# The second modulation of an encoder layer: its last sixth made inside the feed-forward stage

## The chip, the cores and the metric

The kernel runs on one core of a Trainium2 chip. The metric is the device time of one execution in microseconds. Three runs of the kernel before took 1530.63, 1531.85 and 1537.08 us; their median is 1531.85 us.

## What is computed

One layer of a hybrid encoder over a sequence of 1024 tokens of width 1024, all in float32. A conditioning vector `c` gives six vectors of width 1024 through one matrix; two of them scale and shift the input of the mixers, one gates the mixers' output, two scale and shift the input of the feed-forward part, and the last, `g2`, gates its output. Cut to what matters here:

```
cond = silu(c)
sh1, sc1, g1, sh2, sc2, g2 = split(cond @ mod_w + mod_b, 6)
h = rms_norm(x) * (1 + sc1) + sh1
y = concat(ssd(h @ w_in), attention(..), mlstm(..), hyena(..)) @ w_out
x = x + g1 * y
h = rms_norm(x) * (1 + sc2) + sh2
x = x + g2 * ((silu(h @ w_gate) * (h @ w_up)) @ w_down)
return rms_norm(x, final_norm_g)
```

So `g2` is needed only at the very end, when the product with `w_down` is complete, `g1` when `w_out` is prepared, and `sh2`, `sc2` before the feed-forward part.

## The kernel before, in words

The program is written as one sequence of stages, and a scheduler orders each engine's instructions at compile time: it goes by priority (the place in the program, earlier first; what stands under `K.first()`, L226, counts as 2000 places earlier) and by its own estimate of when an instruction's inputs are there. An instruction that is ready may therefore be placed long before the stage in which it is written. At run time every engine and the SP queue, which issues nearly all loads, keep the order that was fixed. A tile that takes the place of another (same tag or slot) waits until the last reader of the old one is done.

The stages, in order of time, are: `start` (the first modulation, the norm of the input) and the Hyena filters; the Hyena convolutions with the SSD and later input projections running beside them on TensorE (`hyena` L819, `project_ssd` L932, lines L493 and L505 for the projections' products); SSD; the mLSTM with the rest of the projections; attention and the output projection; the feed-forward part (`ffn` L1580).

**The second modulation.** The four vectors `g1`, `sh2`, `sc2`, `g2` are 4096 columns of the matrix, cut in eight parts `n` of 512 columns. `modulation2` (L1485) is a generator that `project_ssd` calls between its weight groups, two parts to a call; the fourth call is drained behind it. For each part it loads eight blocks of 128 rows (tile `mxw`, 128x512, 256 KB, two buffers, L1494), multiplies each by its column of `cond` and adds it up on VectorE (L1496 for the first, L1498 for the other seven) in `mxacc` (two buffers), and stores the 128x512 partial sums to memory (`macc`, L1499). Much later, between `project_ml` and `mlstm`, `modulation2_sums` (L1504) loads each `mxacc` again (L1510) and adds over the 128 partitions: for `sh2` and `sc2` by four transposes on TensorE and a reduction (L1514, L1516), for `g1` and `g2` by a product with a matrix of ones (L1527), which leaves the row on all partitions. A bias is added (L1528) and the row stored in `gd` (L1529). `g1` is loaded in `attention` (L1446), `g2` behind the block products (L1712).

**The Hyena stage beside it.** For each of nine frequencies VectorE makes a tile `yk`, TensorE transforms it (`fps`, L790 to L795), VectorE multiplies the result with the filter (L798 to L802, tiles `ta`, `tb`, `rt`), and TensorE transforms it back (`ips`, L804 to L809).

**The five block products.** The products with `w_gate` and `w_up` are computed in a Strassen-like form. A first loop over the 22 hidden blocks makes two block products (`Z`), stored to `psd`. The second loop makes five more: each is 12 matmuls of 128x128 by 128x512, 60 in a block `f`. They go to PSUM tiles `X` and `Y` in turn:

```
product(X, w["T2"], A["S2"], True)
V.tensor_tensor(u, X, p1, op=ALU.add)
product(Y, w["T1"], A["S1"], True)
V.tensor_tensor(v, Y, p1, op=ALU.add)
product(X, w["T3"], A["S3"], False)
V.tensor_tensor(v, X, v, op=ALU.add)
```

The third product adds into the `X` that `u` has read, so it can't begin before VectorE has read it; the same holds for `Y` and the fourth, and for `X` and the fifth. VectorE also makes the weights of block `f + 1` meanwhile (`weights`, L1664).

**Slots.** From attention on, SBUF is a set of numbered slots; a tile names one slot or a ring of several that it takes in turn. Slots 17, 18 and 21 are free in the second loop. `psr`, which holds what the first loop stored, goes round slots 27, 0, 1, 2. The down projection (`part`, L1720) takes slots 17, 18 and 21 first for its weights `wdr`, `wdh`, `wdl`; `g2` lies in slot 0. In the down projection each of eight accumulators takes three matmuls per hidden block: `ah` by `wdh`, `al` by `wdh`, `ah` by `wdl` (L1742).

Of the kernel before, what the change touches and what calls it, by code (L numbers as in the profile page):

```python
# [9 lines left out]
F32 = mybir.dt.float32  # L10
# [7 lines left out]
P = 128  # L18
# [267 lines left out]
def build(nc, tc, d, out, dbg=None, dump=None):  # L286
    K = Net(nc, tc, d, out)
    with ExitStack() as es:
# [43 lines left out]
        K.acr = dp.tile([64, P], F32, name="acr")  # L332
        K.macc = [dp.tile([P, 512], F32, name=f"macc{n}") for n in range(8)]
        K.gd = dp.tile([2, P, D], F32, name="gd")
        K.xd = [dp.tile([P, D], F32, name=f"xd{n}") for n in range(8)]
# [9 lines left out]
        with ExitStack() as e2:  # L345
# [3 lines left out]
            with ExitStack() as e3:  # L349
# [7 lines left out]
                for _ in hf:  # L357
                    pass
            mp = Tags(rpool("m2", right), mxw=2)
            m2 = modulation2(K, mp)  # L360
# [1016 lines left out]
def attention(K, sp, S):  # L1377
# [54 lines left out]
    for a in range(2):  # L1432
        yp = [S.tile([P, 2, 512], F32R, 42 + j, "ny") for j in range(2)]
        ys = [(y[:, 0], y[:, 1]) for y in yp]
        for ti in (2 * a, 2 * a + 1):
            for f in range(2):
                vw = S.tile([120, 4, 256], F32, (40, 41), "nvw")
                rr = NA_ROWS[ti][0]
                for n, cw in enumerate(NA_CH[NA_KIND[ti]]):
                    nc.sync.dma_start(vw[:cw * 40, n], K.vn[f, rr:rr + cw].rearrange("r c e -> (r c) e"))  # L1440
                    rr += cw
                for j in range(2):
                    unit(ti, f, j, vw)
                if ti == 0 and f == 0:
                    K.g1 = S.tile([P, D], F32, 18, "g1")
                    nc.sync.dma_start(K.g1, K.gd[0])  # L1446
            ss = sp.tile([P, 2, 2], F32, "fss", bufs=2)
# [37 lines left out]
def modulation2(K, sp):  # L1485
# [3 lines left out]
    mv = K.mod2  # L1489
    for n in range(8):  # L1490
        acc = sp.tile([P, 512], F32, "mxacc", bufs=2)
        for k in range(NK):
            mt = sp.tile([P, 512], F32, "mxw")
            nc.sync.dma_start(mt, d["modw2"][k * P:(k + 1) * P, n * 512:(n + 1) * 512])  # L1494
            if k == 0:
                V.tensor_scalar_mul(acc, mt, K.cond[:, 0:1])  # L1496
            else:
                V.scalar_tensor_tensor(acc, in0=mt, scalar=K.cond[:, k:k + 1], in1=acc, op0=ALU.mult, op1=ALU.add)  # L1498
        nc.sync.dma_start(K.macc[n], acc)  # L1499
        if n % 2:  # L1500
            yield


def modulation2_sums(K, sp):  # L1504
    nc, d = K.nc, K.d
    V = nc.vector
    mv = K.mod2
    for n in (0, 1, 6, 7, 2, 3, 4, 5):
        acc = sp.tile([P, 512], F32, "mxacc", bufs=2)
        nc.sync.dma_start(acc, K.macc[n])  # L1510
        if 2 <= n < 6:
            ps = K.pm.tile([P, 512], F32, tag="m", name="m2p")
# [8 lines left out]
        else:  # L1521
            m, h = n // 6, n % 2
            hs = slice(h * 512, (h + 1) * 512)
            bb = sp.tile([P, 512], F32, "mxw", name="mxb")
            nc.sync.dma_start(bb, d["modbg"][m:m + 1, hs].broadcast_to([P, 512]))
            ps = K.pm.tile([P, 512], F32, tag="m", name="mgp")
            nc.tensor.matmul(ps, lhsT=K.ones, rhs=acc, start=True, stop=True)  # L1527
            V.tensor_tensor(bb, bb, ps, op=ALU.add)  # L1528
            nc.sync.dma_start(K.gd[m][:, hs], bb)  # L1529

# [49 lines left out]
def ffn(K, sp, S, at):  # L1580
# [100 lines left out]
    with K.first():  # L1681
        ws = [weights(0)]
    for f in range(NF):
        ps1 = S.tile([P, 2, H], F32, (27, 0, 1, 2), "psr")
        nc.sync.dma_start(ps1, K.psd[f])
# [24 lines left out]

    g2 = S.tile([P, D], F32, 0, "g2")
    nc.sync.dma_start(g2, K.gd[1])  # L1712
    fg = S.tile([P, D], F32, 1, "fg")
    nc.sync.dma_start(fg, d["fing"].broadcast_to([P, D]))
    ss = sp.tile([P, 2, 8], F32, "ss")
    for dh in range(2):
# [3 lines left out]
        def part(f2):  # L1720
            raw = S.tile([P, 2, H], F32, (17, 9, 10, 11), "wdr")
            nc.sync.dma_start(raw, d["wd"].rearrange("(a b p) e -> a p b e", b=2, p=P)[f2, :, :, ds])
            wh = S.tile([P, 2, H], F32R, (18, 12, 13, 14), "wdh")
            wl = S.tile([P, 2, H], F32R, (21, 15, 16, 8), "wdl")
            K.split(wh, wl, raw)
# [60 lines left out]
```

## Time and profile before

| | us |
|---|---|
| median of three runs | 1531.85 |
| profiled execution | 1531.33 |
| its span, first to last instruction | 1529.5 |
| TensorE busy in the span | 1412.3 |
| VectorE busy in the span | 1043.3 |
| ScalarE busy in the span | 527.6 |
| GpSimd busy in the span | 91.4 |

The profiled execution took 1.8 us more than its span; what lies outside is the same for any version. PE is TensorE, PEld its weight loads, DVE VectorE, ACT ScalarE, POOL GpSimd, SP the queue that issues loads and stores. A row of a timeline gives start, duration, engine, line, operation, output and inputs, and in brackets how long the engine had been idle before and what ended that. "issue" as releaser means that the engine waited for nothing that the profile shows. The clock is the share of TensorE's full rate that was granted: 1.00 is 2.4 GHz, 0.50 is 1.2 GHz, and a mean between them is a mixture of both.

### The profile page before, as it was taken

What the parts mean: (1) busy time and instruction counts of PE and PEld (TensorE: products, weight loads), DVE (VectorE), ACT (ScalarE), POOL (GpSimd) and SP (SyncE); (2) the same over time, 40 slices, a digit from 0 to 9 for tenths busy, and PEclk for the clock granted to TensorE, in tenths of its full rate; (3) what the DMA queues carried; (4) which work ended last, traced back from release to release, by engine and by line L of the source; (5) the groups of instructions that cost most, each with busy time, mean ns of one, the idle gap of its engine ahead of it and who ended that gap; (6) DMA issues with size and microseconds to landing.
All of it is one profiled execution on the core that took longest, in us unless ns stands there. A gap on an engine that the chain in (4) does not pass through costs nothing.

```text
span 1529.5 us, 19231 instructions
## 1 busy us (share of the span) xinstructions
PE 1412.3 (92%) x6849; PEld 1141.0 (75%) x6849; DVE 1043.3 (68%) x2004; ACT 527.6 (34%) x958; POOL 91.4 (6%) x143
## 2 busy tenths in 40 slices
PE   2589979998998998989989999999999999999997
PEld 0366768876797777867767777888888888888886
DVE  7998977977847684687865476477777766335327
ACT  2522221232242342333456775322222223224222
POOL 2110000000102231230000000000000000000000
PEclk9789999999998999999999999999999999999999
DMA  6534467577653325476426457554444448643402
GB/s 247 194 104 143 128 197 230 185 225 226 190 185 110 105 87 155 125 265 203 154 87 217 150 170 276 201 180 164 148 144 153 149 164 305 222 149 123 153 1 110
DMA packets 134899, 257.02 MB, mean 168 GB/s; under 512 B 24703, under 2 KB 69663, under 8 KB 134804
## 3 DMA queue, kind: packets, MB, share of 16 engines
q1 hardware_dynamic: 111508, 228.50, 45.4%
q10 hardware_dynamic: 22688, 25.99, 4.8%
q0 software_dynamic: 608, 1.31, 0.3%
q8 instruction: 54, 0.88, 0.2%
q14 instruction: 41, 0.34, 0.1%
HBM read 195.17 MB, written 60.59 MB: 167 GB/s over the span
## 4 chain that ended last, share of the span: by engine, by line
PE 74%; DVE 13%; DMA 5%; issue 2%; ACT 2%; POOL 2%; SPq 0%; DVEq 0%; ACTq 0%; POOLq 0%
PE dps L1742 14%; PE X L1603 12%; PE gps L493 9%; PE Z L1603 8%; PE Y L1603 8%; PE gps L505 4%; PE gps L1554 3%; PE nS L1427 2%; PE ops L1554 1%; DMA mxw<-modw 1%; PE nS L1405 1%; DVE wlo L239 1%; PE kps L763 1%; PE mpa L1339 1%; DVE acc L422 1%
## 5 line engine op out<-in xcount | busy, mean ns | idle before, releaser
L1742 PE MATMUL dps<-wdh,ah 128*128 128x512 f32 x352 | 136.9, 389 | 0.0
L1742 PE MATMUL dps<-wdh,al 128*128 128x512 f32 x352 | 136.9, 389 | 0.0
L1742 PE MATMUL dps<-wdl,ah 128*128 128x512 f32 x352 | 136.9, 389 | 0.0
L493 PE MATMUL gps<-hhi,whi 128*128 128x512 f32 x320 | 130.7, 408 | 3.8 <-ACT nt L529 3.8
L493 PE MATMUL gps<-hlo,whi 128*128 128x512 f32 x320 | 129.6, 405 | 0.0
L493 PE MATMUL gps<-hhi,wlo 128*128 128x512 f32 x320 | 129.0, 403 | 0.0
L1603 PE MATMUL Z<-hp,wgh 128*128 128x512 f32 x352 | 95.4, 402 | 1.9 <-ACT ps L1658 1.6
L239 DVE TENSOR_TENSOR al<-ar,ah 128x1024 fp32r<-128x1024 f32 x44 | 53.4, 1222 | 47.9 <-ACT ah L233 47.9
L505 PE MATMUL gps<-whi,hhi 128*128 128x256 f32 (+1 forms) x256 | 77.5, 303 | 1.5 <-ACT z L529 1.5
L1603 PEld LDWEIGHTS Z<-hp,wgh 128*128 128x128 f32 x352 | 63.7, 188 | 19.8 <-ACT ps L1658 5.3
L505 PE MATMUL gps<-whi,hlo 128*128 128x256 f32 (+1 forms) x256 | 77.2, 302 | 0.0
L505 PE MATMUL gps<-wlo,hhi 128*128 128x256 f32 (+1 forms) x256 | 77.1, 301 | 0.0
L1742 PEld LDWEIGHTS dps<-wdl,ah 128*128 128x128 f32 x352 | 66.1, 188 | 13.8
L1742 PEld LDWEIGHTS dps<-wdh,al 128*128 128x128 f32 x352 | 66.1, 188 | 13.7
L1742 PEld LDWEIGHTS dps<-wdh,ah 128*128 128x128 f32 x352 | 66.1, 188 | 13.6
L493 PEld LDWEIGHTS gps<-hhi,whi 128*128 128x128 f32 x320 | 60.6, 189 | 19.5 <-ACT nt L529 5.0
L493 PEld LDWEIGHTS gps<-hhi,wlo 128*128 128x128 f32 x320 | 60.5, 189 | 13.8 <-issue 1.6
L233 ACT CAST ah<-ar 128x1024 fp32r<-128x1024 f32 x44 | 45.7, 1048 | 72.5 <-PE dps L1742 42.7
L493 PEld LDWEIGHTS gps<-hlo,whi 128*128 128x128 f32 x320 | 60.6, 189 | 12.4 <-issue 0.8
L1603 PE MATMUL X<-A,t4s 128*128 128x512 f32 x264 | 63.4, 389 | 0.0
L239 DVE TENSOR_TENSOR wdl<-wdr,wdh 128x1024 fp32r<-128x1024 f32 x22 | 26.9, 1224 | 53.1 <-ACT wdh L233 53.1
L1498 DVE SCALAR_TENSOR_TENSOR mxacc<-mxw,cond,mxacc 128x512 f32<-128x512 f32 x56 | 42.0, 750 | 29.2 <-DMA mxw<-modw 28.9
(500 smaller groups left out, 3240.5 us busy)
## 6 DMA issues: line engine op xcount, KB each, us to landing
wg<-wg SPq DMA_DIRECT2D x44, 512.0 KB
ar<-ad SPq DMA_DIRECT2D x44, 512.0 KB
mxw<-modw SPq DMA_DIRECT2D x64, 256.0 KB
raw<-w_in SPq DMA_DIRECT2D x28, 512.0 KB
psd<-ps SPq DMA_DIRECT2D x22, 512.0 KB
psr<-psd SPq DMA_DIRECT2D x22, 512.0 KB
wu<-wu SPq DMA_DIRECT2D x22, 512.0 KB
wdr<-wd SPq DMA_DIRECT2D x22, 512.0 KB
```

The lines of the kernel that those rows point to most:

```text
L233: nc.scalar.copy(hi, src)
L239: e.tensor_tensor(lo, src, hi.bitcast(F32), op=ALU.subtract)
L422: V.scalar_tensor_tensor(acc, in0=w, scalar=c, in1=acc, op0=ALU.mult, op1=ALU.add)
L493: nc.tensor.matmul(ps, lhsT=w[:, k, c], rhs=x[k][:, t], start=n == 0, stop=n == len(seq) - 1)
L505: nc.tensor.matmul(ps, lhsT=x[k][:, t], rhs=w[:, k, :N], start=n == 0, stop=n == len(seq) - 1)
L763: nc.tensor.matmul(ps, lhsT=tab[:, la], rhs=y[:, 0], start=True, stop=not cx)
L1339: nc.tensor.matmul(pa[:, 2 * j + dr], lhsT=sds[dr][:, h], rhs=va[:, h], start=True, stop=True)
L1427: nc.tensor.matmul(pb[:, 448:512], lhsT=pT[:w * 40, n], rhs=vw[:w * 40, n, c:c + 64], start=n == 0, stop=n == len(chunks) - 1)
L1498: V.scalar_tensor_tensor(acc, in0=mt, scalar=K.cond[:, k:k + 1], in1=acc, op0=ALU.mult, op1=ALU.add)
L1554: K.nc.tensor.matmul(ps, lhsT=l, rhs=r, start=n == 0, stop=n == 5)
L1603: nc.tensor.matmul(ps, lhsT=w[a][:, k], rhs=x[k][b], start=start and n == 0, stop=n == 11, skip_group_check=not start)
L1742: nc.tensor.matmul(acc[i], lhsT=x[:, ts], rhs=m, start=f == 0 and n == 0, stop=f == NF - 1 and n == 2)
```

## The change

The two parts `n` of `g2` leave `modulation2` and `modulation2_sums`; six parts remain. In these, `mxw` has three buffers in place of two and `mxacc` one in place of two (the same SBUF in all), and the parts are summed in the order 0 to 5. `g2` is now made in `ffn`, written at block `f == 4` of the second loop: eight loads of 128x1024 (512 KB) go round slots 18 and 21, VectorE adds them up in slot 17, the bias is loaded into the same ring, and two products with the ones matrix and two additions leave `g2` in slot 17, where it stays. Its way through memory (`macc`, `gd`) is gone. In the down projection the first slots of the rings are 18, 21 and 0 in place of 17, 18 and 21.

```diff
-            mp = Tags(rpool("m2", right), mxw=2)
+            mp = Tags(rpool("m2", right), mxw=3)
@@ modulation2 and modulation2_sums
-    for n in range(8):
-        acc = sp.tile([P, 512], F32, "mxacc", bufs=2)
+    for n in range(6):
+        acc = sp.tile([P, 512], F32, "mxacc")
...
-    for n in (0, 1, 6, 7, 2, 3, 4, 5):
-        acc = sp.tile([P, 512], F32, "mxacc", bufs=2)
+    for n in range(6):
+        acc = sp.tile([P, 512], F32, "mxacc")
@@ new
+def weighted_rows(K, S, c0, acc, slots):
+    nc, d = K.nc, K.d
+    for k in range(NK):
+        mt = S.tile([P, D], F32, slots, "mwt")
+        nc.sync.dma_start(mt, d["modw2"][k * P:(k + 1) * P, c0:c0 + D])
+        if k == 0:
+            nc.vector.tensor_scalar_mul(acc, mt, K.cond[:, 0:1])
+        else:
+            nc.vector.scalar_tensor_tensor(acc, in0=mt, scalar=K.cond[:, k:k + 1], in1=acc, op0=ALU.mult, op1=ALU.add)
+
+def modulation_g2(K, S, slots):
+    nc, d = K.nc, K.d
+    acc = S.tile([P, D], F32, slots[0], "g2")
+    weighted_rows(K, S, 3 * D, acc, slots[1:])
+    bb = S.tile([P, D], F32, slots[1:], "g2b")
+    nc.sync.dma_start(bb, d["modbg"][1:2].broadcast_to([P, D]))
+    for h in range(2):
+        hs = slice(h * 512, (h + 1) * 512)
+        ps = K.pg.tile([P, 512], F32, tag="g", name="mgp")
+        nc.tensor.matmul(ps, lhsT=K.ones, rhs=acc[:, hs], start=True, stop=True)
+        nc.vector.tensor_tensor(acc[:, hs], bb[:, hs], ps, op=ALU.add)
+    return acc
@@ ffn, the second loop and the down projection
     for f in range(NF):
+        if f == 4:
+            g2 = modulation_g2(K, S, (17, 18, 21))
...
-    g2 = S.tile([P, D], F32, 0, "g2")
-    nc.sync.dma_start(g2, K.gd[1])
...
-            raw = S.tile([P, 2, H], F32, (17, 9, 10, 11), "wdr")
+            raw = S.tile([P, 2, H], F32, (18, 9, 10, 11), "wdr")
...
-            wh = S.tile([P, 2, H], F32R, (18, 12, 13, 14), "wdh")
-            wl = S.tile([P, 2, H], F32R, (21, 15, 16, 8), "wdl")
+            wh = S.tile([P, 2, H], F32R, (21, 12, 13, 14), "wdh")
+            wl = S.tile([P, 2, H], F32R, (0, 15, 16, 8), "wdl")
```

## Rows read from the trace of the kernel before

**Rows 1.** The page, part 1: busy time of each engine, share of the span, instructions.

```profile
PE 1412.3 (92%) x6849; PEld 1141.0 (75%) x6849; DVE 1043.3 (68%) x2004; ACT 527.6 (34%) x958; POOL 91.4 (6%) x143
```

**Rows 2.** Windows of time by stage: PE, PEld, DVE, ACT, POOL; clock; DMA share; GB/s.

```profile
219.00:378.00 159.00, 145.62 (x705) 122.27 (x704) 123.86 (x225) 40.48 (x67) 0.00 (x0) 0.98 0.69 219
378.00:433.00 55.00, 51.61 (x233) 41.85 (x232) 41.15 (x81) 13.76 (x42) 6.13 (x11) 1.00 0.66 203
...
585.00:607.00 22.00, 17.51 (x109) 14.85 (x109) 7.02 (x14) 3.52 (x8) 2.00 (x4) 0.92 0.75 227
...
1000.00:1100.00 100.00, 100.00 (x443) 82.63 (x442) 73.22 (x102) 23.86 (x30) 0.00 (x0) 1.00 0.47 159
...
1280.00:1290.00 10.00, 10.00 (x46) 8.28 (x45) 7.82 (x8) 4.40 (x5) 0.00 (x0) 1.00 0.93 301
```

**Rows 3.** Tile mxw, whole span: count, min/median/max ns, first and last start, then waits.

```profile
L1494 SPq DMA_DIRECT2D mxw<-modw x64: 327/328/862, 219.9 to 423.4; - x64
L1498 DVE SCALAR_TENSOR_TENSOR mxacc<-mxw,cond,mxacc x56: 743/751/754, 225.6 to 428.4; 128x512 f32<-128x512 f32 x56
L1496 DVE TENSOR_SCALAR mxacc<-mxw,cond x8: 477/483/491, 224.0 to 395.5; 128x512 f32<-128x512 f32 x8
...
  DMA mxw<-modw: 32.2, 25
```

**Rows 4.** Waits of VectorE, 378 to 433 us: total, times, longest.

```profile
DVE mxacc L1498 <- DMA mxw<-modw: 9.2, 7, 2.6
```

**Rows 5.** Waits of TensorE, 219 to 433 us: total, times, longest.

```profile
PE fps L790 <- issue: 5.8, 4, 3.4
PE ips L804 <- DVE rt L801: 3.9, 3, 2.2
PE ips L804 <- issue: 2.8, 3, 1.4
```

**Rows 6.** Timeline of VectorE, 366 to 369 us: start, duration, idle before.

```profile
366.32 0.75 DVE L1498 SCALAR_TENSOR_TENSOR mxacc<-mxw,cond,mxacc 128x512 f32<-128x512 f32 x1 [3.92 <-DMA mxw<-modw]
...
368.86 0.42 DVE L802 TENSOR_TENSOR rt<-ta,tb 128x256 f32<-128x256 f32 x1
```

**Rows 7.** Timeline of TensorE, 366 to 370 us.

```profile
368.99 0.70 PE L804 MATMUL ips<-rt,tai 128*128 128x256 f32 x2 [2.17 <-DVE rt L801]
```

**Rows 8.** Tile mxacc: the products with the ones matrix.

```profile
L1527 PE MATMUL mgp<-mxacc,ones x8: 592/594/692, 585.9 to 593.1; 128*128 128x512 f32 x8
```

**Rows 9.** Timeline of the SP queue, 597 to 600 us.

```profile
597.33 0.32 SPq L1510 DMA_DIRECT2D mxacc<-macc  x1
...
599.54 18.29 SPq L1277 DMA_DIRECT2D mkv<-mvk  x8
```

**Rows 10.** Timeline of TensorE, 602 to 603 us.

```profile
602.17 0.72 PE L1514 MATMUL m2p<-ident,mxacc 128*128 128x128 f32 x4 [2.18 <-DMA mxacc<-macc]
```

**Rows 11.** Groups by shape on VectorE: count | busy, mean ns | idle before, releaser.

```profile
L1670 DVE TENSOR_TENSOR t<-wu,wg 128x512 f32<-128x512 f32 x22 | 15.2, 692 | 9.4 <-DMA wu<-wu 9.3
...
L1701 DVE TENSOR_TENSOR uv<-Y,uv 128x512 f32<-128x512 f32 x22 | 15.2, 691 | 43.8 <-PE Y L1603 43.8
...
L1542 DVE SCALAR_TENSOR_TENSOR wor<-wor,pc,g 128x1024 f32<-128x1024 f32 x8 | 10.2, 1275 | 0.0
...
L1480 DVE TENSOR_SCALAR x<-x,x1r 128x1024 f32<-128x1024 f32 x8 | 5.5, 742 | 0.0
```

**Rows 12.** Timeline of VectorE, the end of the block products.

```profile
1280.86 0.69 DVE L1705 TENSOR_TENSOR psr<-X,psr 128x512 f32<-128x512 f32 x1
...
1283.72 0.69 DVE L1707 TENSOR_TENSOR a<-uv,psr 128x512 f32<-128x512 f32 x1
```

**Rows 13.** Timeline of TensorE, the first product of the down projection.

```profile
1279.90 0.39 PE L1742 MATMUL dps<-wdh,ah 128*128 128x512 f32 x1
```

**Rows 14.** Tile wdl, whole span.

```profile
L239 DVE TENSOR_TENSOR wdl<-wdr,wdh x22: 1216/1226/1227, 994.0 to 1476.8; 128x1024 fp32r<-128x1024 f32 x22
```

More of the change, by code (lines that the diff above doesn't have):

```diff
@@ L332, in build @@
         K.acr = dp.tile([64, P], F32, name="acr")
-        K.macc = [dp.tile([P, 512], F32, name=f"macc{n}") for n in range(8)]
-        K.gd = dp.tile([2, P, D], F32, name="gd")
+        K.macc = [dp.tile([P, 512], F32, name=f"macc{n}") for n in range(6)]
+        K.gd = dp.tile([P, D], F32, name="gd")
         K.xd = [dp.tile([P, D], F32, name=f"xd{n}") for n in range(8)]
@@ L1445, in attention @@
                     K.g1 = S.tile([P, D], F32, 18, "g1")
-                    nc.sync.dma_start(K.g1, K.gd[0])
+                    nc.sync.dma_start(K.g1, K.gd)
             ss = sp.tile([P, 2, 2], F32, "fss", bufs=2)
@@ L1507, in modulation2_sums @@
     mv = K.mod2
-    for n in (0, 1, 6, 7, 2, 3, 4, 5):
-        acc = sp.tile([P, 512], F32, "mxacc", bufs=2)
+    for n in range(6):
+        acc = sp.tile([P, 512], F32, "mxacc")
         nc.sync.dma_start(acc, K.macc[n])
-        if 2 <= n < 6:
+        if n >= 2:
             ps = K.pm.tile([P, 512], F32, tag="m", name="m2p")
@@ L1521, in modulation2_sums @@
         else:
-            m, h = n // 6, n % 2
-            hs = slice(h * 512, (h + 1) * 512)
+            hs = slice(n * 512, (n + 1) * 512)
             bb = sp.tile([P, 512], F32, "mxw", name="mxb")
-            nc.sync.dma_start(bb, d["modbg"][m:m + 1, hs].broadcast_to([P, 512]))
+            nc.sync.dma_start(bb, d["modbg"][0:1, hs].broadcast_to([P, 512]))
             ps = K.pm.tile([P, 512], F32, tag="m", name="mgp")
@@ L1528, in modulation2_sums @@
             V.tensor_tensor(bb, bb, ps, op=ALU.add)
-            nc.sync.dma_start(K.gd[m][:, hs], bb)
+            nc.sync.dma_start(K.gd[:, hs], bb)
+def weighted_rows(K, S, c0, acc, slots):
[19 more added lines that the diff above has]
+    return acc
 def load_wo(K, S, ct, tiles):
```

## The prediction

> **What bounds the kernel now.** I read the page's busy times first: TensorE works 92% of the span, VectorE 68% [rows 1], so time is lost or won where TensorE stands still, and VectorE counts where TensorE waits for it. Then the windows by stage [rows 2]. From 219 to 433 us, where the second modulation runs, TensorE is busy 145.6 + 51.6 of 159 + 55 us: it stands idle for 16.8 us, and in the first of these windows its mean clock is 0.98, so that 159 x 0.02 / 0.5 = 6.4 us ran at the lower level. In the block products (the window of 1000 to 1100 us) TensorE is never idle: 443 matmuls in 100 us, one per 0.226 us, at full clock; VectorE is busy for 73.2 us of the 100. This is the contrast on which the change turns: work leaves a stage where TensorE waits for VectorE and enters one where TensorE is full.
>
> Who waits for whom is read from the tile `mxw` [rows 3]: VectorE waited 32.2 us, in 25 pieces, for its loads; 9.2 us of that lie behind 378 us [rows 4], where the two parts of `g2`, the last, are multiplied. The waits of TensorE in the stretch [rows 5] are mostly for `yk` and `rt`, tiles that VectorE makes. One case shows the link: VectorE, which keeps its order, waits 3.92 us for an `mxw`, ends the two halves of `rt` only at 369.0 us [rows 6], and TensorE, idle for 2.17 us, starts at that moment [rows 7].
>
> **The Hyena stage.** Two of eight parts leave: 16 loads, 2 x 0.483 + 14 x 0.750 = 11.5 us of VectorE's work [rows 3], two stores, and the 9.2 us of waits [rows 4]. For the 48 loads that stay, 32.2 - 9.2 = 23.0 us of waits are left. With a third buffer a load is issued three multiplications ahead in place of two, and I let a late landing be paid once in three loads: 23.0 x 2/3 = 15.3, a gain of 7.7 us (between 0, if the loads are late by what they share, and 23.0). The single accumulator costs: five times the first multiplication of a part must wait until the store of the part before has landed. The trace shows no such wait; the nearest row is a load of the same size, which took 224.0 - 219.9 = 4.1 us from issue to use [rows 3]. The bounds are 0 and 5 x 4.1 = 20.5 us; since the scheduler has other work for VectorE at hand I take 1 us each, 5 us. VectorE thus waits 9.2 + 7.7 - 5 = 11.9 us less. What does TensorE get of it? The waits of rows 5 add up to 5.8 + 3.9 + 2.8 = 12.5 us for the 32.2 us, 0.39 for one; 11.9 x 0.39 = 4.6 us. Of the two stretches at the lower clock (3.2 us each, so 1.6 us lost in each) I count one as gone: **-6.2 us**. At best all idle time and all of the lower clock go: -16.8 - 3.2 = -20 us. At worst the accumulator costs its 20.5 us: (16.9 - 20.5) x 0.39 = +1.4 us. The 11.5 us of work that VectorE is spared I count at nothing more, because TensorE is idle for only 3.4 us behind 378 us [rows 2]: projections fill it.
>
> One rule here goes the other way from my third buffer's worth. The rows show 4.1 us for a load of 256 KB in a stretch where the DMA engines are busy 69% [rows 2, 3]. The Trainium skill, "DMA: Bandwidth & Descriptors", section "Anatomy of one DMA — SWDGE (gpsimd) path", fits 2.0 us plus the bytes at 436 GB/s for one transfer on that path, which would be an estimated 2.6 us here. By that price the loads would hardly be late at all, and the buffer would bring almost nothing; the measured 4.1 us decides, and no sum below uses the other.
>
> **The sums.** Two of four products with the ones matrix go; each is two records of 0.594 us [rows 8], so 2.4 us of TensorE. In the window of 585 to 607 us TensorE is idle for 4.5 us, so part of this falls into time that is waited away anyhow; half is counted, -1.2. Two reloads, two additions and two bias loads go too. Against that stands the single buffer: a reload can be issued only when the products or transposes have read the tile, and one took 602.17 - 597.33 = 4.8 us from issue to use [rows 9, 10], TensorE being idle for the last 2.18 us of it. Five reloads in series are 24 us, against 602.2 - 585.9 = 16.3 us from the first part to the seventh of eight now [rows 8, 10], and on the SP queue the first loads of the mLSTM (`mkv`) stand right behind the last reload [rows 9]. The bounds are -4.5 and +4. I take **-1.2 us**, as if the series just balanced the two loads that are gone.
>
> **The block products.** What moves in is eight loads of 512 KB, one of 512 KB for the bias, one multiplication (0.742 us), seven multiply-adds (1.275 us each), two additions (0.69 each): 11.0 us of VectorE by the like forms [rows 11], and the two products, 4 x 0.594 = 2.4 us of TensorE [rows 8]. TensorE is full here, so the products cost **+2.4 us**. A block is 60 x 0.226 = 13.5 us, of which VectorE is busy 9.9 and free 3.6; so the 11.0 us need at least three blocks. The scheduler gives the old work of earlier blocks first choice and fills the rest, but a multiply-add whose load is late holds everything behind it. The cover: between the first product into `X` and the third lies the second, 12 x 0.226 = 2.7 us, and reading `X` takes 0.69 of it; so about 2.0 us are left, which agrees with the 43.8 us over 22 blocks that VectorE waits at this place [rows 11]. A multiply-add of 1.28 us fits; one that also waits over 0.7 us doesn't. Late loads exist here already: VectorE waits 9.3 us in all for `wu` [rows 11], with the DMA engines 47% busy. If four of the eight wait for the mean of the Hyena stage (32.2 / 25 = 1.3 us), TensorE loses 0.6 each: **+2.5 us**. The bounds: 0, and with every load waiting for the worst 3.9 us [rows 6], 8 x (3.9 + 1.3 - 2.0) = 26 us. If the bias or the last multiply-add is late, TensorE waits before the ones products; this is inside that bound.
>
> **The turn to the down projection.** The first `wdl` was made at 994.0 us [rows 14], long before use. It now takes slot 0, which the `psr` of block 21 holds until L1707 has read it, at 1284.4 us [rows 12]; with its 1.22 us it is there at 1285.6. The third matmul of the down projection wants it at 1280.35, two places behind the first [rows 13]. In the order of before this would be 5.3 us of idle TensorE. But of the first hidden block 16 matmuls need no `wdl` (14 more than those two, 3.2 us), and the scheduler knows that the slot is late and can put them first. What remains is 2.1 us at the times of before, nothing if L1705 to L1707 aren't queued behind the splits of `al`; I take about half, **+1.1 us**, bounds 0 and 5.3. The `g2` load that went out in the busiest window (DMA share 0.93) [rows 2] is gone, at no gain, since TensorE is full there.
>
> **The sum.** -6.2 - 1.2 + 2.4 + 2.5 + 1.1 = -1.4 us. The profiled execution took 1531.33 us, 0.5 less than the median of the three runs; the forecast is 1531.33 - 1.4 = 1529.9 us. About 0.5%, 7.7 us, is what a measurement of this kernel can tell from no change: I forecast no difference.
>
> **Rivals.**
> *VectorE's relief counts in full.* VectorE is spared 11.9 us of waits and 11.5 us of work; with its waits it has hardly a pause in this stage (123.9 + 41.2 us of work and 32.2 of waits in 214). If three quarters of TensorE's 16.8 us and of the lower clock's 3.2 go, that is -15, and with g2 fully hidden (+2.4) and the rest as above 1531.3 - 15 - 1.2 + 2.4 + 1.1 = 1518.6 us. For it: nearly every wait of rows 5 stands behind VectorE. Against: from 378 us on there is little left to win. Chance 0.24.
> *Late g2 loads stop the block products.* The one mechanism that makes it slower: a multiply-add in VectorE's fixed order waits for its 512 KB over 0.7 us beyond its place, and the next product into `X` or `Y` waits with it. From two buffers and a DMA load that rises above 47% I can see 1.6 us for each of eight loads, 13 us in place of 2.5: 1540.4 us. For it: the same pattern stalls TensorE in the Hyena stage. Against: 3.6 us of pause in each block, and 512 KB loads that are over with a few blocks. Chance 0.21.
> *One accumulator makes the sums a chain.* The sums take their +4 and the accumulators' turnover its 20.5 us: 1531.3 + 1.4 + 4 + 6 = 1542.7 at the very worst, and with half of these excesses 1536. For it: rows 9 and 10. The Trainium skill, "Trainium Kernel Development and Optimization", section "Best Practices", advises double-buffering to overlap transfers with work, which speaks against this half of the change; the 2.18 us of idle time at a reload that already has a second buffer agrees that it isn't free. Chance 0.10.
> That g2 isn't made in block 4 but as soon as slots 18 and 21 are free is likely (the first `wdl` was made 286 us early [rows 14]); it changes the place, not the price.
>
> **How the numbers follow.** The forecast has 0.45 and, with its own terms' spread, 1524 to 1537. The range takes in the first rival less its best bounds and the second: 1516 to 1542. Faster by over 0.5% needs the first rival: 0.24. Slower by over 0.5% needs the second: 0.21. The rest, forecast and third rival, is 0.55.
>
> **What would show it.** Right: VectorE's waits for `mxw` about 18 to 20 us, TensorE idle for some 11 us between 219 us and the end of the Hyena stage; in the block products a loss of two to five us against 443 matmuls per 100 us, all within a few blocks; a gap of at most 2 us before the first `wdl` product. Wrong: TensorE gaps behind `mwt` loads of more than 8 us in all, or a Hyena stage that ends 10 us earlier with TensorE still full.

## The result, and the profile after

The changed kernel takes 1541.17 us (median of 12 runs), the kernel before beside it 1531.03: a ratio of 1.0064, interval 1.0039 to 1.0088, which is 9.8 us slower (10.1 by the two medians). I had forecast no difference. Below, a ratio is turned into microseconds by 1531 us; a trace is one execution, a ratio rests on all runs of a kernel. The profiled execution took 1540.6 us, its span 1538.8. Lines behind the sums are 26 higher than before (the block products are L1629, the down projection L1768).

The page's first part, and the windows by stage (columns as in [rows 2]):

```profile
PE 1420.6 (92%) x6849; PEld 1147.1 (75%) x6849; DVE 1042.0 (68%) x1996; ACT 527.4 (34%) x958; POOL 89.0 (6%) x143
```

```profile
219.00:378.00 159.00, 147.74 (x724) 125.18 (x723) 128.13 (x233) 40.83 (x69) 0.00 (x0) 0.98 0.71 226
378.00:433.00 55.00, 53.45 (x254) 44.50 (x253) 34.23 (x72) 18.72 (x53) 6.15 (x11) 1.00 0.36 111
585.00:607.00 22.00, 20.50 (x217) 18.80 (x216) 9.66 (x22) 5.58 (x16) 8.29 (x14) 1.00 0.79 223
640.00:720.00 80.00, 70.31 (x358) 53.76 (x358) 62.02 (x143) 28.66 (x51) 11.53 (x15) 0.91 0.68 232
1000.00:1100.00 100.00, 99.23 (x433) 80.74 (x433) 80.69 (x111) 24.69 (x30) 0.00 (x0) 1.00 0.55 186
1280.00:1290.00 10.00, 7.31 (x33) 5.63 (x31) 8.68 (x11) 7.48 (x8) 0.00 (x0) 1.00 0.87 305
```

Against [rows 2], TensorE works 4.0 us more in the first two windows and 3.0 us more from 585 to 607 us: up to here the change gains. In the block products ten matmuls are missing between 1000 and 1100 us, and behind 1280 us TensorE, which never stood still there, is idle for 2.7 us. The window of 640 to 720 us, the turn from the mLSTM to the output projection, was not among my rows. Before it read:

```profile
640.00:720.00 80.00, 74.10 (x404) 58.10 (x404) 64.19 (x149) 28.46 (x48) 15.98 (x21) 0.96 0.66 226
```

TensorE has lost 3.8 us of work there, and its mean clock fell from 0.96 to 0.91: a larger share at the lower of its two levels (1.2 in place of 2.4 GHz). Between 785 and 980 us, a stretch that ends with the first loop (`Z`), it fell too, before and then after:

```profile
785.00:980.00 195.00, 189.18 (x897) 148.71 (x896) 110.12 (x243) 120.68 (x215) 0.00 (x0) 0.98 0.55 189
785.00:980.00 195.00, 189.62 (x889) 148.62 (x889) 109.28 (x242) 119.22 (x214) 0.00 (x0) 0.97 0.56 192
```

The starts of some instructions show how a lead is won and lost (us; L505 makes the last input projections, `mpa` L1339 the last products of the mLSTM, `wor` is the output projection's first weight load):

| | before | after | lead |
|---|---|---|---|
| last Hyena gate `z` (L842) | 427.3 | 419.8 | 7.5 |
| sums, first product with ones (`mgp`) | 585.9 | 578.9 | 7.0 |
| mLSTM, first product (L1286) | 608.2 | 599.3 | 8.9 |
| last projection (L505) | 649.5 | 644.3 | 5.2 |
| last product of the mLSTM (L1339) | 674.9 | 666.7 | 8.2 |
| first `wor` load | 662.5 | 656.6 | 5.9 |
| output projection, first product | 675.0 | 669.8 | 5.2 |
| output projection, last `gps` product | 785.2 | 783.7 | 1.5 |
| `X`, first product | 977.8 | 977.9 | -0.1 |
| `X`, last product | 1279.7 | 1283.3 | -3.6 |
| down projection, first product | 1279.9 | 1283.5 | -3.6 |
| down projection, last product of `ah` by `wdh` | 1518.6 | 1527.9 | -9.3 |

So three things are to be explained: 8 to 9 us won and lost again by 978 us (3.0 between the end of the mLSTM and the output projection, 3.7 in the output projection, 1.6 behind it), 3.5 us lost beside `X`, 5.7 us lost in the down projection.

**The loads.** Tile `mxw` after, to be held against [rows 3]:

```profile
L1494 SPq DMA_DIRECT2D mxw<-modw x48: 327/328/443, 222.7 to 355.0; - x48
...
  DMA mxw<-modw: 8.2, 9
  DMA macc<-mxacc: 2.9, 2
...
DMA to landing us min/median/max: 2.7/3.2/4.5
```

VectorE waits 8.2 us in place of 32.2, and 2.9 us for the single accumulator. A load took 3.2 us in the median from issue to landing; the prediction's 4.1 us ran to the first use.

**The sums.** Tile `mxacc`: the transposes before, then both kinds of product after, to be held against [rows 8]:

```profile
L1514 PE MATMUL m2p<-ident,mxacc x16: 270/273/415, 596.7 to 606.2; 128*128 128x128 f32 x16
```

```profile
L1526 PE MATMUL mgp<-mxacc,ones x4: 592/594/667, 578.9 to 583.4; 128*128 128x512 f32 x4
L1514 PE MATMUL m2p<-ident,mxacc x16: 272/273/302, 587.0 to 599.1; 128*128 128x128 f32 x16
```

Eight sums with two accumulators took 606.2 - 585.9 = 20.3 us, six with one take 599.1 - 578.9 = 20.2 us: what two sums less give, the single accumulator takes. The sums begin 7.0 us earlier, so the gain of the Hyena stage reaches them. The mLSTM follows the last sum by 0.2 us (2.0 before) and starts 8.9 us earlier.

**The turn of the mLSTM.** Waits of TensorE, 640 to 725 us (total, times, longest), before and then after:

```profile
PE gps L1554 <- DVE yl L239: 5.3, 3, 3.4
PE mpa L1339 <- ACT msd L1324: 0.3, 1, 0.3
PE gps L1554 <- ACT yh L233: 0.2, 1, 0.2
```

```profile
PE gps L1580 <- DVE yl L239: 4.6, 3, 2.5
PE gps L1580 <- ACT wowh L233: 2.8, 1, 2.8
PE gps L1580 <- ACT yh L233: 1.2, 1, 1.2
...
```

The mLSTM's last product now starts 3.1 us before the output projection's first (0.1 before): TensorE waits for `wowh`, the split of the weights whose load went out only at 656.6 us, 12.3 us behind the last projection (13.0 before).

**The block products.** All waits of TensorE between 978 and 1279 us are one:

```profile
PE Y L1629 <- DVE uv L1725: 0.8, 1, 0.8
```

g2's multiplications ran from 988.2 to 1019.2 us, in blocks 0 to 3, and VectorE waited for `mwt` once, 1.9 us.

**The turn to the down projection**, timeline of TensorE, then VectorE, then ScalarE, and last ScalarE before:

```profile
1286.92 0.39 PE L1768 MATMUL dps<-wdh,al 128*128 128x512 f32 x1
1291.05 2.84 PE L1768 MATMUL dps<-wdl,ah 128*128 128x512 f32 x8 [3.74 <-DVE wdl L239]
1293.69 0.63 PE L1768 MATMUL dps<-wdh,ah 128*128 128x512 f32 x1
```

```profile
1285.32 2.46 DVE L239 TENSOR_TENSOR al<-ar,ah 128x1024 fp32r<-128x1024 f32 x2 [0.17 <-ACT ah L233]
1288.03 0.69 DVE L1735 TENSOR_TENSOR a<-uv,psr 128x512 f32<-128x512 f32 x1 [0.25 <-ACT psr L1734]
1288.64 2.35 DVE L239 TENSOR_TENSOR wdl<-wdr,wdh 128x1024 fp32r<-128x1024 f32 x2
```

```profile
1284.23 1.06 ACT L233 CAST ah<-ar 128x1024 fp32r<-128x1024 f32 x1 [1.15 <-DMA ar<-ad]
...
1287.38 0.62 ACT L1734 ACTIVATE psr<-psr 128x512 f32<-128x512 f32 x1
```

```profile
1279.87 1.06 ACT L233 CAST ah<-ar 128x1024 fp32r<-128x1024 f32 x1 [0.40 <-DMA ar<-ad]
...
1283.02 0.64 ACT L1706 ACTIVATE psr<-psr 128x512 f32<-128x512 f32 x1
```

Before, the last reader of `psr` ran at 1283.72 us [rows 12], 3.8 us behind the first product of the down projection; now it runs at 1288.03, 4.5 us behind it. ScalarE makes its input at 1287.38, 3.9 us behind the first product (3.1 before), in the same order of casts as before; the load of `ar` that the first of these casts waits for came later (1.15 us of idle time in place of 0.40). Behind the reader VectorE makes two `wdl`, 2.35 us, and TensorE goes on only behind the second. The 16 products that need no `wdl` are gone by 1287.3; then TensorE is idle for 3.74 us, and the products behind take 0.63 us in place of 0.39, at the lower clock.

### The profile page after: what moved, and what is told of

It reads as the page before. It is cut to its first block, busy times and chain, and to the rows that moved or that the text cites. A ratio compares the mean times of both kernels' runs of the same rounds, so it can differ in the third digit from the quotient of the medians.

```text
span 1538.8 us, 19192 instructions
## 1 busy us (share of the span) xinstructions
PE 1420.6 (92%) x6849; PEld 1147.1 (75%) x6849; DVE 1042.0 (68%) x1996; ACT 527.4 (34%) x958; POOL 89.0 (6%) x143
## 4 chain that ended last, share of the span: by engine, by line
PE 55%; DVE 4%; DMA 2%; ACT 1%; issue 1%; POOL 0%; DVEq 0%; SPq 0%; ACTq 0%; POOLq 0%
PE dps L1768 14%; PE X L1629 11%; PE Z L1629 8%; PE Y L1629 7%; PE gps L1580 4%; PE nS L1427 2%; PE nS L1405 1%; PE ops L1580 1%; PE mpa L1339 1%; PE gps L505 1%; PE nT L1419 1%; DMA mxacc<-macc 1%; DVE xn L1796 1%; PE gps L493 1%; PE mpi L1333 1%
## 5 line engine op out<-in xcount | busy, mean ns | idle before, releaser
L1768 PE MATMUL dps<-wdl,ah 128*128 128x512 f32 x352 | 136.9, 392 | 3.7 <-DVE wdl L239 3.7
L1768 PE MATMUL dps<-wdh,ah 128*128 128x512 f32 x352 | 137.4, 390 | 0.0
L1768 PE MATMUL dps<-wdh,al 128*128 128x512 f32 x352 | 137.3, 390 | 0.0
L1629 PE MATMUL Z<-hp,wgh 128*128 128x512 f32 x352 | 97.1, 406 | 0.9 <-ACT ps L1684 0.7
L1768 PEld LDWEIGHTS dps<-wdl,ah 128*128 128x128 f32 x352 | 66.6, 189 | 18.2 <-DVE wdl L239 4.2
L1629 PEld LDWEIGHTS Z<-hp,wgh 128*128 128x128 f32 x352 | 64.3, 190 | 19.2 <-ACT ps L1684 4.6
L505 PE MATMUL gps<-whi,hhi 128*128 128x256 f32 (+1 forms) x256 | 76.9, 300 | 1.5 <-ACT z L529 1.5
L1768 PEld LDWEIGHTS dps<-wdh,ah 128*128 128x128 f32 x352 | 66.4, 189 | 13.8
L1768 PEld LDWEIGHTS dps<-wdh,al 128*128 128x128 f32 x352 | 66.4, 189 | 13.8
L505 PE MATMUL gps<-wlo,hhi 128*128 128x256 f32 (+1 forms) x256 | 76.0, 297 | 0.0
L505 PE MATMUL gps<-whi,hlo 128*128 128x256 f32 (+1 forms) x256 | 75.9, 296 | 0.0
L1629 PE MATMUL X<-A,t4s 128*128 128x512 f32 x264 | 63.5, 389 | 0.0
L1629 PEld LDWEIGHTS X<-A,t4s 128*128 128x128 f32 x264 | 49.5, 188 | 10.5 <-issue 0.3
```

Of the source, the lines that this page charges most:

```text
L505: nc.tensor.matmul(ps, lhsT=x[k][:, t], rhs=w[:, k, :N], start=n == 0, stop=n == len(seq) - 1)
L1629: nc.tensor.matmul(ps, lhsT=w[a][:, k], rhs=x[k][b], start=start and n == 0, stop=n == 11, skip_group_check=not start)
L1768: nc.tensor.matmul(acc[i], lhsT=x[:, ts], rhs=m, start=f == 0 and n == 0, stop=f == NF - 1 and n == 2)
```

## The experiments

**The turn to the down projection.** `e_slots` is the kernel before with the slots of the change, `e_turn` the changed kernel with slot 0 kept out of the ring of `psr`; there `g2` lies in slot 0, and the down projection begins with slots 17, 18 and 21 as before.

```diff
-    g2 = S.tile([P, D], F32, 0, "g2")
+    g2 = S.tile([P, D], F32, 17, "g2")
...
-            wl = S.tile([P, 2, H], F32R, (21, 15, 16, 8), "wdl")
+            wl = S.tile([P, 2, H], F32R, (0, 15, 16, 8), "wdl")
```

> The kernel before with the change of slots in the down projection alone: rings 18, 21 and 0 for wdr, wdh and wdl, g2 loaded into slot 17 as before from memory. Theory: the slot alone makes the gap; 5 to 6 us slower than the kernel before (1.0037), with an idle TensorE of 3 to 4 us before the first wdl product and a stretch at the lower clock behind it. Rival: the gap needs the g2 work in the block products; then under 1.5 us.

```diff
-            g2 = modulation_g2(K, S, (17, 18, 21))
-        ps1 = S.tile([P, 2, H], F32, (27, 0, 1, 2), "psr")
+            g2 = modulation_g2(K, S, (0, 17, 18))
+        ps1 = S.tile([P, 2, H], F32, (27, 1, 2), "psr")
```

> The changed kernel with one thing mended: psr goes round three slots (27, 1, 2), g2 takes slot 0, its loads 17 and 18, and the down projection has its old rings 17, 18, 21. Theory: the turn to the down projection costs what the two traces show, 5.7 us (the last product of the down projection is 9.3 us later than before, the first 3.6). Then this is 5 to 6 us faster than the changed kernel, 1.0025 times the kernel before, and the first wdl product comes two places behind the first product. Rival: the turn only passes on a delay that VectorE carries there anyway; then the gap moves to another tile and under 2 us are gained.

`e_slots`: 1.0029 [1.0007, 1.0050], 4.4 us. Waits of TensorE, 1278 to 1300 us:

```profile
PE dps L1742 <- DVE wdl L239: 3.5, 1, 3.5
```

From the first to the last `wdh` product of the down projection it needs 1524.8 - 1280.9 = 243.9 us; the kernel before 238.7, the changed one 244.4. `e_turn` is back at 238.7, with TensorE full from 1280 to 1400 us:

```profile
1280.00:1400.00 120.00, 120.00 (x531) 99.38 (x530) 50.48 (x50) 36.73 (x43) 0.00 (x0) 1.00 0.58 198
```

By the traces the term is 5.2 us (`e_slots`) and 5.7 us (the changed kernel), by the runs 4.4 us for `e_slots` and 2.6 us between the changed kernel and `e_turn`, where 5 to 6 were expected; the runs allow a few us to either side. That the slot alone makes the gap is shown. `e_turn` is still slower than the kernel before: 1.0047 [1.0020, 1.0074], not 1.0025.

**g2 in the block products.** `e_nog2` is `e_turn` with the bias alone loaded into g2's slot.

```diff
-    weighted_rows(K, S, 3 * D, acc, slots[1:])
...
+    nc.sync.dma_start(acc, d["modbg"][1:2].broadcast_to([P, D]))
```

> The changed kernel with the turn to the down projection mended (slot 0 kept out of psr's ring, as in e_turn), and g2 not made in the feed-forward stage (its slot holds the bias alone: the eight loads, the multiplications and the two products are left out). Against e_turn it prices g2 in the block products. Theory: 443 matmuls or more per 100 us from 1000 us on, 3 to 4 us less than e_turn, 1534.5 to 1535.5 us, still 4 us above the kernel before, because the lead is lost ahead of Z. Rival (g2 costs nothing there, and all the loss lies ahead): 1538 us. Rival two (g2 is the whole loss): 1530 us.

1.0023 [1.0000, 1.0045], 3.7 us less than `e_turn` by intervals that overlap; the 443 matmuls per 100 us are back:

```profile
1000.00:1100.00 100.00, 100.00 (x443) 82.63 (x442) 74.68 (x105) 24.64 (x29) 0.00 (x0) 1.00 0.47 163
```

The theory held here. What is left, 3.5 us by the runs and 1.8 us in its trace (`X` begins at 979.6 us, 977.8 before), arises ahead of the block products, in a kernel that has less to do there.

**The buffers.** `e_g2move` is `e_turn` with two load buffers and two accumulators; `e_bufs` is the kernel before with three and one (the edit below; `e_g2move` has its reverse).

```diff
-            mp = Tags(rpool("m2", right), mxw=2)
+            mp = Tags(rpool("m2", right), mxw=3)
...
-        acc = sp.tile([P, 512], F32, "mxacc", bufs=2)
+        acc = sp.tile([P, 512], F32, "mxacc")
```

> g2 made in the block products with the mended slots, but two load buffers and two accumulators for the six parts that stay. Theory: moving g2 takes 3.6 us in the block products (two products with the ones matrix of 1 us each, a stall of 0.8, some tenths more) and gives back 2 to 5 us in the Hyena stage: 0.998 to 1.001 of the kernel before. Rival: the moved work alone brings the Hyena stage's gain in full; then 0.995 or less. The difference from the mended kernel with three buffers and one accumulator is what these are worth.

> The kernel before with three load buffers and one accumulator, all eight parts left in place. Theory: VectorE waits less for mxw (15 us or less in place of 32), but the sums become a chain and TensorE gains at most 3 us: 0.998 to 1.001. Rival: the single accumulator delays the mLSTM and costs 4 us or more: 1.0026 or above.

`e_g2move`: 1.0098 [1.0068, 1.0128]; `e_bufs`: 1.0113 [1.0068, 1.0158]. Both theories miss; for `e_bufs` the rival came true. With the single accumulator eight sums in series end at 618.1 us (606.2 before), the mLSTM starts 10 us later, the projections are over at 624.2 and the mLSTM runs on alone to 690 us. The third buffer does what it should (waits for `mxw`: 11.5 us of 32.2 with eight parts, 8.2 in place of 21.6 with six). With six parts the single accumulator makes the sums longer as well; `e_g2move`, with two, needs 595.7 - 583.7 = 12.0 us for them, against 20.2:

```profile
L1526 PE MATMUL mgp<-mxacc,ones x4: 592/594/697, 583.7 to 586.0; 128*128 128x512 f32 x4
L1514 PE MATMUL m2p<-ident,mxacc x16: 272/273/300, 587.6 to 595.7; 128*128 128x128 f32 x16
```

Yet `e_turn`, with three buffers and one accumulator, is 7.8 us faster than `e_g2move` (1.0047 against 1.0098): its sums begin at 575.9 us, 7.8 us earlier. So with six parts the pair of changes pays, with eight it costs 17 us.

**Relief for nothing.** If the lead is lost on the way, taking work out of the Hyena stage without putting it anywhere should bring little. `e_six`:

```diff
-    for n in range(8):
+    for n in range(6):
...
-    for n in (0, 1, 6, 7, 2, 3, 4, 5):
+    for n in range(6):
...
-    nc.sync.dma_start(g2, K.gd[1])
+    nc.sync.dma_start(g2, d["modbg"][1:2].broadcast_to([P, D]))
```

> The kernel before with the two parts of g2 left out (neither loaded, nor multiplied, nor summed; the output is gated by the bias alone), everything else, buffers and slots too, as it was. It says what the relief of the Hyena stage and of the sums is worth when nothing is paid for it. Theory (the lead is handed back between 640 and 785 us): the Hyena stage ends 4 to 8 us earlier, the mLSTM's first products come 4 to 8 us earlier, but Z at 813 us is not over 2 us earlier, and the time is 1528 to 1532 us, at most 3 us below the kernel before. Rival (the relief counts, and the change loses only by what it adds): Z and the end 6 us or more earlier, 1520 to 1525 us.

`e_one` has `for k in range(1)` in `modulation2` besides.

> The same, and of the six parts that stay only the first of eight row blocks is loaded and multiplied (seven eighths of the products with the conditioning vector are left out); the sums remain. VectorE is spared some 36 us of work and all waits for mxw. Theory: TensorE is full in the Hyena stage (idle under 6 us between 219 and 433 us), the stage ends 10 to 15 us earlier, and of that at most 5 us are left at the end: 1525 to 1530 us. Rival (what the stage gains is kept): 1515 to 1520 us.

`e_six`: 1.0078 [1.0052, 1.0104], 12 us slower; my theory had said 0 to 3 faster. `e_one`: 1.0016 [0.9997, 1.0035] (median 1534.72 us), where I had expected 1525 to 1530 us. Windows for `e_one` (its traced execution took 1539.85 us, the longest of its 12):

```profile
219.00:433.00 214.00, 206.06 (x1015) 174.92 (x1015) 140.49 (x283) 63.60 (x130) 6.15 (x11) 0.98 0.49 155
585.00:640.00 55.00, 55.00 (x384) 45.70 (x384) 37.96 (x113) 17.85 (x38) 14.55 (x24) 0.97 0.35 93
640.00:720.00 80.00, 61.07 (x339) 49.02 (x338) 36.29 (x112) 24.54 (x59) 3.85 (x6) 0.79 0.62 208
```

In the Hyena stage TensorE works 8.8 us more than before (197.2 us), and between 640 and 720 us it works 13 us less, at a clock of 0.79. The mLSTM is over at 648.2 us, the last projections at 663.1, and the output projection's weights are loaded from 681.5 us on. TensorE waits there first for `nk`, a tile that attention loads:

```profile
PE nS L1405 <- DMA nk<-kt: 11.8, 1, 11.8
```

So relief does go through the stage (the mLSTM's first product comes at 576.7 us, 608.2 before), and all of it is paid back behind the mLSTM. For `e_six` most of that lies in the output projection itself, from its first product (677.4 us) to its last (795.2): 117.8 us, against 110.2 before. Windows before, then `e_six`:

```profile
675.00:785.00 110.00, 104.39 (x513) 79.06 (x513) 84.71 (x211) 45.56 (x100) 4.09 (x5) 0.97 0.49 160
675.00:785.00 110.00, 101.95 (x466) 76.39 (x467) 79.08 (x189) 43.68 (x95) 3.65 (x3) 0.89 0.49 159
```

The mean clock is 0.89 in place of 0.97, which is 110 x 0.08 / 0.5 = 18 us more at the lower level; if TensorE had work in all of it, an estimated 9 us are lost by the clock.

Three runs take `e_six` apart: `e_sum6` leaves out the sums alone, `e_mod6` the Hyena part alone, `e_ctl` only reorders the sums.

```diff
@@ e_sum6: modulation2_sums (and g2 from the bias); e_ctl: range(8)
-    for n in (0, 1, 6, 7, 2, 3, 4, 5):
+    for n in range(6):
@@ e_mod6: modulation2
+        if n >= 6:
+            V.memset(acc, 0.0)
-        for k in range(NK):
+        for k in range(NK if n < 6 else 0):
```

> The kernel before with all eight parts computed and stored in the Hyena stage, but only six summed, in the order 0 to 5 (the sums of g2 and its two products are left out, its slot holds the bias alone). Its instruction order differs from the kernel before only around the sums and in the mLSTM. Theory A (the relief of the Hyena stage is what goes wrong downstream): the mLSTM's first products come 3 to 6 us earlier, 1527 to 1532 us. Theory B (an mLSTM that starts earlier leaves its tail, which has nothing beside it, longer, and that costs): 1535 us or more.

> The kernel before with the two parts of g2 neither loaded nor multiplied in the Hyena stage (their accumulators are set to zero and stored, so that g2 is the bias alone), and all eight sums as before. Theory A: the Hyena stage ends 4 to 8 us earlier, TensorE has 1 to 3 us less work left at 433 us, and this is lost by 785 us: 1536 to 1542 us, as with both left out (1541.7). Theory B: the sums stand where they stood, the lead is kept: 1526 to 1530 us.

> The kernel before with the eight sums in the order 0 to 7 (g2's two last) in place of 0, 1, 6, 7, 2 to 5, and nothing else: the same work, another order of a few dozen instructions around 585 to 625 us. Theory C (this kernel's order is a tuned one, and any change of it before the output projection costs some us): 1534 to 1540 us. Theories A and B: within 2 us of the kernel before, since neither the Hyena stage nor the start of the mLSTM moves by much.

`e_sum6` 0.9999 [0.9977, 1.0021] and `e_ctl` 1.0008 [0.9990, 1.0026]: no difference. So neither an mLSTM that starts 3 to 4 us earlier (603.8 and 605.4 us) nor these two other orders of the sums cost anything here. `e_mod6`: 1.0036 [1.0019, 1.0052], slower, as theory A said. Its wait at the turn, in the timeline of TensorE:

```profile
675.04 1.11 PE L1339 MATMUL mpa<-mkv,msd 128*128 128x65 f32 x8
685.59 1.65 PE L1556 MATMUL gps<-wowh,yh 128*128 128x512 f32 x3 [9.44 <-ACT yh L233]
```

Where the kernels stand at this turn (starts in us), with the mean clock of the span over all runs of each (for the kernel before, those beside the experiments):

| | last projection | mLSTM's last product | first `wor` load | output's first product | ratio | clock |
|---|---|---|---|---|---|---|
| before | 649.5 | 674.9 | 662.5 | 675.0 | 1 | 0.974 |
| `e_ctl` | 633.7 | 673.2 | 648.3 | 670.8 | 1.0008 | 0.971 |
| `e_sum6` | 630.6 | 669.8 | 646.1 | 667.5 | 0.9999 | 0.971 |
| after | 644.3 | 666.7 | 656.6 | 669.8 | 1.0064 | 0.968 |
| `e_turn` | 642.4 | 674.1 | 654.9 | 677.3 | 1.0047 | 0.966 |
| `e_mod6` | 662.3 | 675.9 | 671.4 | 685.6 | 1.0036 | 0.971 |
| `e_six` | 652.0 | 674.4 | 663.2 | 677.4 | 1.0078 | 0.967 |
| `e_one` | 663.1 | 648.2 | 681.5 | 690.2 | 1.0016 | 0.966 |

In every row the load goes out 9 to 18 us behind the last projection, and the first product follows 9 to 23 us later. In the three rows of ratio 1 it is there when the mLSTM ends or before; in the five with less work in the Hyena stage TensorE waits 3 us and more behind the mLSTM. The ratio does not follow the length of this gap: `e_one`, with the longest, has saved the most, and TensorE's wait for the first `wowh` is 2.79 us in the changed kernel, `e_turn`, `e_nog2`, `e_six` and `e_g2move` alike, whose ratios go from 1.0023 to 1.0098.

The runs with less work in the Hyena stage differ from the kernel before in a second thing: the scheduler gives them another order. In the traces 264 of the mLSTM's 432 products stand ahead of the last projection before, 291 in the changed kernel (and in `e_turn`), 298 in `e_six`, 340 in `e_mod6`, all 432 in `e_one`. No run here has the relief in the order of before, so that the relief and the new order aren't told apart.

**Moving the turn.** `e_fill` puts 24 products that nobody reads into the gap of `e_turn`; `e_wob` gives the output projection's first loads and splits first choice, in the kernel before.

```diff
+    ps = K.pm.tile([P, 512], F32, tag="m", name="fill")
+    for i in range(24):
+        nc.tensor.matmul(ps, lhsT=gr[:, 7 * P:], rhs=oneh[:, 0], start=True, stop=True)
```

> e_turn with 24 products more at the end of the mLSTM, into a PSUM tile that nobody reads, 24 x 0.213 us = 5.1 us at full clock, put where TensorE otherwise stands idle for 2.8 and 2.5 us before the output projection's first weights. Theory (idle time at this turn is followed by a stretch at half clock, and this costs 3 to 15 us by chance): the mean clock of 640 to 720 us is 0.97 or more, and the time is 1532 to 1536 us, with less scatter than e_turn. Rival (the order and the late weights cost the time, the clock has nothing to do with it): the clock falls as before, 1538 to 1541 us.

```diff
+                    with K.first():
+                        nc.sync.dma_start(K.g1, K.gd[0])
...
+    with K.first() if first else nullcontext():
```

> The kernel before with the loads and splits of the first output round (wor, yr, g1) given first choice. In its order the first products of the output projection stand among the last two chunks of the mLSTM and no longer behind them. If TensorE's loss between 640 and 720 us comes from the mLSTM's tail, which has nothing beside it, this fills some of it: the idle 6.6 us from 673 to 685 us fall to 3 or less and the stretch at half clock behind them goes, 1524 to 1528 us. If the waits for yl and wowh are what counts there, they only move: 1529 to 1532 us.

Both miss. `e_fill`: 1.0066 [1.0042, 1.0089]. The filler ran where it was meant to (674.6 to 680.0 us), but the clock had fallen before, while the mLSTM's last chunks ran: 0.79 over 640 to 680 us with TensorE busy for 38.99 of the 40 us. So it says nothing against a part of the clock in the loss, and shows that idle time in that gap is not what lowered it here. `e_wob`: 1.0082 [1.0058, 1.0106]; its first output products stand inside the mLSTM and hold its last ones up to 683.9 us (674.9), with one wait for `yh` of 5.2 us.

The last three runs write the projections ahead of the mLSTM, in the kernel before, in `e_six` and in `e_turn`.

```diff
             modulation2_sums(K, mp)
+            project_na(K)
             mlstm(K, Tags(rpool("ml", right), va=2))
-            project_na(K)
```

> The kernel before with the projections of the neighbourhood attention written ahead of the mLSTM, so that they come first and the output projection's first products fill the mLSTM's tail. The base for the next two. The mLSTM begins some 20 us later and the output projection's first weights are there before it ends: no wait of over 2 us for wowh or yh. 1528 to 1545 us; both theories are open on this one.

> The same edit on the kernel before without g2 (e_six). Theory (the relief is lost at the turn, because the last projections end late there and the first weights of the output projection wait for their memory): with that turn no longer bound by the projections the relief is kept, and it is 3 to 8 us faster than e_first_b. Rival (the relief is lost elsewhere, or any other order costs): no faster than e_first_b, or slower by 5 us and more, as e_six against the kernel before.

> The same edit on the changed kernel with its turn to the down projection mended (e_turn). Theory: slower than e_first_s by what g2 costs in the block products, 4 to 5 us, and thus within 3 us of e_first_b, where e_turn was 8 us slower than the kernel before. Rival: 6 us or more slower than e_first_b.

`e_first_b` 1.0079 [1.0060, 1.0098], `e_first_s` 1.0061 [1.0038, 1.0084], `e_first_t` 1.0057 [1.0032, 1.0081]. The projections end at 618.9, 616.7 and 612.7 us, `wor` loads at 635.6, 633.4 and 630.0. All three are slower than the kernel before, but among them the order has turned round: taking g2 out costs 12 us in the old order and gives some 3 in this one, and the change costs 7 us there and none here. The intervals overlap, so that the 3 us are not shown to be a gain; what is shown is that the same relief costs nothing in this order. It doesn't show that the late weights were the cause: `e_first_b` itself, with no relief, has lost 12 us, and its clock is as low as that of the relieved kernels (0.968 over its runs, `e_first_s` and `e_first_t` 0.966). `e_first_t` was expected to be 4 to 5 us behind `e_first_s` and isn't. No version here beats the kernel before.

## Why the prediction was wrong

**The Hyena stage (-6.2): right up to the sums, wrong in what it was worth.** Of 20.3 us of waits that I left to VectorE (15.3 for loads, 5 for the accumulator) 8.2 + 2.9 remain, and TensorE gains 4.0 us of work; the clock stays at 0.98. The sums begin 7.0 us earlier. The step that failed is the entry of this gain in the sum as time off the end: the path from the mLSTM to the block products stood in it at nothing, and I had read no row of it. The lead is 8.9 us at the mLSTM's start and 8.2 us at its end, 5.2 us at the output projection's first product, 1.5 us at its last, and -0.1 us at `X`. In the trace TensorE waits 2.8 us for the first `wowh`, and the clock is lower: 0.95 in place of 0.98 in the mean of 640 to 785 us, and 0.97 in place of 0.98 from 785 to 980 us. The trace has 13.7 us at the lower level in the first of these windows (6.8 before) and 10.2 in the second (6.8), an estimated 4 to 5 us lost. One or two us I can't place. The nearest run for this term alone is `e_mod6`: not -6.2 but +5.5 us; in its trace the loss begins with the wait for `yh` (9.44 us), behind projections that end 12.8 us later than before, while in the changed kernel they end 5.2 us earlier. So the relief is lost behind the mLSTM in both, but not by the same wait.

**The sums (-1.2): the sign was right, and it is lost too.** My grounds held: the series of six reloads through one accumulator balances the two sums that are gone (20.2 against 20.3 us). What the stage gains is 1.8 us between the last sum and the mLSTM. The rival of the chain holds with eight parts (34.5 us in `e_bufs`) and with six (20.2 against 12.0 us in `e_g2move`), but as a price of the single accumulator, not as the reason of the loss.

**The block products (+4.9): right.** 3.5 us in the trace and 3.7 by the runs. The ones products (1.9 us) and 0.8 us of waiting make 2.7 of it; the rest I can't place. Late g2 loads, the rival whose time of 1540.4 us is near the measured one, are not the cause, so that nearness is chance: VectorE waited for one of eight, 1.9 us. The multiplications spread over four blocks.

**The turn to the down projection (+1.1, bounds 0 and 5.3): the mechanism was right, the size wrong.** It is 5.7 us. I saw the slot, the reader and the 16 products that need no `wdl`; at the times of before that left 2.1 us, and I then took half without a row for it. The measured gap is 3.74 us: the reader comes 0.7 us later behind the first product, because a load holds up ScalarE, which makes its input and whose queue I had not looked at; and TensorE goes on behind two `wdl`, 2.35 us, where I had counted one of 1.22. Behind the gap products took 0.63 us in place of 0.39 at the clock's lower level, and that is most of the other 2 us.

The sum then reads: +5.7 for the turn, +3.5 for g2, and 0.1 for everything ahead, 9.3 us of span. By the runs it is 2.6 (the changed kernel against `e_turn`), 3.7 and 3.5, each uncertain by 3 to 6 us.

The clock is a rival to late weights as the cause of what is lost ahead of `X`, and by the estimate for `e_six` the larger one there. The kernel before has a mean clock of 0.974 over its runs, the changed one 0.968, `e_turn` 0.966: 2 x 0.006 x 1540 = some 18 us more at the lower level for the changed kernel. If TensorE had work in all of it, that would be an estimated 9 us, as much as the lead. In its trace only part of this lies between 585 us and the turn to the down projection; what the lower clock at the two ends of the span costs no run shows.

What stays open: whether it is the relief or the new order that brings the loss, what lowers the clock behind the mLSTM, why the last projections end later in `e_mod6`, `e_six` and `e_one`, and what holds the `wor` load behind them. That they give up the memory it lands in, or that their stores stand behind the mLSTM's activations on ScalarE's queue, is argued and was not tried.

## What to carry to other kernels

A lead that one stage wins counts at the end only if every later stage hands it on. Here it came through the sums and the whole mLSTM, and was gone two stages later, at a wait for the next stage's weights and at a lower clock. So follow a lead to the next points that wait for something else, and count it only if they move too. A slot that passes from one stage's ring to the next stage's first tile must be priced with the queues of all engines in front of its last reader, and with every instruction between that reader and the product that waits. And try the relief for nothing first: one run with the work left out (`e_six`) would have shown that, in the order that the scheduler makes of it, there was nothing to win.

## What the hardware showed unexpectedly

TensorE's clock fell at the end of the mLSTM in a stretch where its records show it busy, and for very different lengths in kernels that run the same order of instructions there. Windows of TensorE alone (busy, clock, DMA share, GB/s), before, after and `e_turn`:

```profile
640.00:660.00 20.00, 20.00 (x133) 1.00 0.54 162
660.00:680.00 20.00, 16.26 (x106) 1.00 0.83 319
```

```profile
640.00:660.00 20.00, 18.94 (x123) 1.00 0.78 251
660.00:680.00 20.00, 14.09 (x65) 0.74 0.67 256
```

```profile
640.00:660.00 20.00, 18.97 (x101) 0.82 0.91 286
660.00:680.00 20.00, 16.57 (x61) 0.50 0.37 145
```

`e_turn`, with the same order on TensorE as the changed kernel, came to this place 2 us earlier and left it 7.5 us later (first output product 677.3 against 669.8 us). What ran ahead of the fall were mostly the mLSTM's narrow products, 128x65, 64x130 and 64x128, with no projections beside them; but `e_sum6` ran 39 us of that too, at a clock of 1.00 from 640 to 668 us. So narrow products alone do not explain it. It goes with the scatter between runs of one kernel: the fastest of `e_turn`'s 12 runs, 1531.11 us, has a mean clock of 0.970, the slowest, 1548.06 us, of 0.959. That is 2 x 0.011 x 1540 = 34 us more at the lower level, an estimated 17 us if TensorE had work in all of it, and the slow run is 17.0 us longer. The kernel before, beside it, went from 1526.77 to 1541.19 us.
